# One encoder layer on one core: small steps moved between engines and within the order of the work

## The chip, the core and the metric

The kernel runs on one core of one Trainium2 chip. A core has a matrix engine (TensorE, PE in the profile), a vector engine (VectorE, DVE), a scalar engine (ScalarE, ACT), a general engine (GpSimd, POOL) and SyncE (SP), which here only issues transfers. Each engine takes its instructions in the order in which they were queued and stops at the first one whose operands are not ready. Data lies in SBUF (128 partitions) and the results of matmuls in PSUM. The metric is the device time in microseconds of one execution; it is 901.49 us, the median of 901.3, 901.49 and 904.68.

## The reference

One layer (DEPTH 1) over 512 tokens and 16 learned meta tokens, width 1024:

- h = RMSNorm(x), then one projection h @ W_in gives u (512 columns), q (1024), k and v (256 each) and two gates (1024 each).
- u goes through a bidirectional diagonal complex state-space model with 32 groups of 16 channels and 64 states per direction, then GELU and a gated linear unit.
- q and k are normalized per head of 64 (RMSNorm), rotated by position tables and used in attention: 16 query heads share 4 key heads, the softmax goes over all 528 tokens.
- out = x + W_out(sigmoid(gate_ssm) * (y_ssm @ P_ssm) + sigmoid(gate_attn) * (y_attn @ P_attn)); then an MLP with relu squared (4096 wide) and a last RMSNorm. The meta tokens are dropped at the end.

## The kernel before, in words

All matmuls are in float32 accuracy by a split: each operand is a high part (`split`, line 101: a cast on one engine) plus a low part (the difference, a subtraction on another engine), and `mm3` (line 157) adds three products. So each weight tile needs a DMA, a cast and a subtraction before PE can use it.

`load_w` (line 108) does this for one weight tile. It has two buffers each for the raw tile `wf`, the high part `wh` and the low part `wl`. `W_ENG[0]` says for load number i which engines work: ScalarE casts, and the low part is a subtraction on VectorE or GpSimd, or, where the second entry is None, it is made by ScalarE (negated copy, line 122) and an accumulating DMA that GpSimd issues (line 123). From the state stage on (line 504) the first eight loads go by DMA and the later ones by VectorE.

The stages, in order of time in the profile:

1. Start, to about 60 us. `xnorm` (line 459) normalizes the four 128-row tiles of x and the 16 meta rows: ScalarE squares and sums, VectorE and ScalarE make the reciprocal root (`rsqrt`), VectorE scales (line 479), PE transposes (line 483) and both engines split the result into hTh and hTl. It is called for tile 0, for tile 1 with the meta rows, and for tiles 2 and 3. PE meanwhile projects k (kv_t[0], five row blocks, of which the last is the meta rows), the first 128 columns of u, then v. VectorE also computes the parameters of the state space model (`p_exp`, `p_sincos`); the first instruction of that block (line 568) masks `dd`, the table made from the input ssm_d, which is first read in `ssm_build` (line 785).
2. State projection and scan, about 60 to 226 us. `ssm_build`, `ssm_run` and `ssm_out` make 8 rounds; between them `pump` (line 278) emits matmuls of the fill tasks: the rest of u, the first gate and three tiles of the second gate.
3. Gated linear unit, keys, first two query groups and the projection of y_ssm, about 226 to 300 us. `norm_rope` (line 923) normalizes and rotates k or one group of four query heads; `k_stacks` (line 975) transposes the keys and writes high and low parts Kh and Kl. Each key head is written twice, into partitions 0 to 63 and 64 to 127, since `scores` multiplies a tile that holds the high part of a query head in one half and the low part in the other.
4. Attention, about 300 to 476 us. Per head and block of 128 queries: scores on PE, maximum on VectorE, exp on ScalarE, reciprocal on VectorE, scaling on GpSimd (line 1134), transposes on PE, split on ScalarE and VectorE, and the product with v. The third and fourth query groups and five tiles of the second gate are background work in this stage; the steps of `norm_rope` are then queued in `bgq` and taken out a few at a time (`bg_pop`).
5. From about 476 us: output projections and the MLP.

The order on each engine comes from a scheduler that simulates the whole program: each instruction has a priority by its place in the program, changed by `tc.high_priority`, and `tc.issue_after` holds an instruction behind another one of its engine. A moved line therefore changes the priority of its instructions, and the simulated order of others may change with it. The task list itself is planned by costs written in the code: `pump` advances a clock by 0.33 or 0.65 per step, a task runs when `ready()` holds, and when a task starts, the next ready one has its weights loaded.

The steps that matter here: `rsqrt` (line 165) has a branch for 16 or more columns that starts from an integer trick on VectorE and makes three Newton steps of three VectorE instructions each (lines 179 to 181). In attention `norm_rope` calls it with 16 columns (128x16). The fill list of stage 3 is line 1091, and it runs until line 1092 is satisfied; the list for attention is line 1176. The key halves are written here:

```
for src, cs_ in ((ps, slice(NM, L)), (pm_, slice(L, L + NM)), (pm_, slice(0, NM))):
    for d_ in (a, b_):
        split(src[a], Kh[d_, g, cs_], Kl[d_, g, cs_], S, V)
```

Of the kernel before, what the change touches and what calls it, by code (L numbers as in the profile page):

```python
# [10 lines left out]
F32 = mybir.dt.float32  # L11
# [3 lines left out]
ALU = mybir.AluOpType  # L15
# [9 lines left out]
G = 32  # L25
P16 = 16
# [44 lines left out]
def hybrid_block(ctx, tc, x, meta, w_in, w_glu, w_ssm, w_attn, w_out, w_m1, w_m2,  # L71
# [3 lines left out]
    V, S, Q, PE = nc.vector, nc.scalar, nc.gpsimd, nc.tensor  # L75
# [12 lines left out]
    ident = const.tile([128, 128], F32, name="ident")  # L88
# [3 lines left out]
    W_ENG = [lambda i: (S, Q if i % 2 else V)]  # L92
# [8 lines left out]
    def split(src, h, l, eh, el):  # L101
        a = copy_on(eh, h, src)
        b = el.tensor_tensor(out=l, in0=src, in1=h.bitcast(F32), op=ALU.subtract)  # L103
        return [a.ins, b.ins]
# [57 lines left out]

    rs_ins = []

    def rsqrt(v, n, p=128, name="rs"):

        y, a, t = [small.tile([128, n], F32, tag=f"rs_{c}{n}", bufs=4 if n < 16 else 1 if n > 16 else 2, name=name + c)[:p]
                   for c in "yat"]
        if n < 16:
            rs_ins[:] = [S.activation(out=y, in_=v, func=AF.Abs_reciprocal_sqrt).ins]  # L170
            V.tensor_scalar(out=a, in0=v, scalar1=-0.5, scalar2=None, op0=ALU.mult)
        else:
            V.tensor_scalar(out=t.bitcast(I32), in0=v.bitcast(I32), scalar1=1, scalar2=None,
                            op0=ALU.logical_shift_right)
            V.tensor_scalar(out=y.bitcast(I32), in0=t.bitcast(I32), scalar1=-1.0,
                            scalar2=1597463007.0, op0=ALU.mult, op1=ALU.add)
            V.tensor_scalar(out=a, in0=v, scalar1=-0.5, scalar2=None, op0=ALU.mult)
        for _ in range(1 if n < 16 else 3):
            V.tensor_tensor(out=t, in0=y, in1=y, op=ALU.mult)
            V.tensor_tensor(out=t, in0=t, in1=a, op=ALU.mult)  # L180
            V.scalar_tensor_tensor(out=y, in0=t, scalar=1.5, in1=y, op0=ALU.add, op1=ALU.mult)
        return y
# [55 lines left out]
    dd = sp.tile([P16, G, P16], F32, name="dd")  # L238
# [37 lines left out]
    fill_q, clk, brk, owed, ordered = [], [0.0], [False], [0.0], [False]  # L276
# [180 lines left out]
    xn_ins, xs_ins = [], []  # L457
# [35 lines left out]
    with tc.issue_after(xn_ins[1]):  # L493
        for _ in range(len(bgq) // 2):
            bgq.pop(0)[1]()
        with tc.issue_after(xs_ins[1]):
            bg_flush()
    xnorm((1,), True)
    xnorm((2, 3), False)
    x_st.close()  # L500
    fill_q += [kv_t[0], t_u(0, uTs), kv_t[1]]
    drain()
    nw0 = wcount[0]
    W_ENG[0] = lambda i: (S, V if i - nw0 > 7 else None)


    def tt(a, b, op, o=None):
        o = ptile() if o is None else o
        V.tensor_tensor(out=o, in0=a, in1=b, op=op)
        return o  # L510
# [54 lines left out]
        return sin, cos  # L565

    with tc.issue_after(xn_ins[1]):
        V.tensor_tensor(out=dd, in0=dd, in1=ident[:P16, None, :P16].to_broadcast([P16, G, P16]), op=ALU.mult)
        dt = p_exp(ldt)
        lre = ts(are, -1e-4, ALU.min)  # L570
    mag = p_exp(tt(lre, dt, ALU.mult))
    sn, cs = p_sincos(tt(aim, dt, ALU.mult))
    GP = [128, G, P16]
    sc1, sc2, sc3, sc4 = [pp.tile(GP, F32, name=f"sc{j}") for j in range(4)]
    sc5, sc6 = [gfl[:, 4 * G * j:4 * G * j + 4 * G] for j in range(2)]
# [288 lines left out]
    for i in range(8):  # L864
        c, b = divmod(i, 2)
# [38 lines left out]
    Kh = kp.tile([128, NKV, L + NM], F32R, name="Kh")  # L904
    Kl = kp.tile([128, NKV, L + NM], F32R, name="Kl")
# [17 lines left out]
    def norm_rope(nt, qk, steps=None, buf=0):  # L923
# [6 lines left out]
        st = small.tile([128, 5, 4], F32, tag="st", name="st")[:, :nt]  # L930
# [3 lines left out]
        rr = []  # L934
# [4 lines left out]

        def rs():  # L940
            V.tensor_scalar(out=st, in0=st, scalar1=1.0 / HD, scalar2=EPS, op0=ALU.mult, op1=ALU.add)
            rr.append(rsqrt(st.rearrange("p t h -> p (t h)"), nt * 4).rearrange("p (t h) -> p t h", t=nt))

        def sin_(h):
            n = h.stop - h.start
# [29 lines left out]
    def k_stacks(kr):  # L975
        pm2 = asc()
        for gp in range(2):
            ps = atr()
            pm_ = pm2[:, 16 * gp:16 * gp + 16]
            for t in range(5):  # L980
                n = 128 if t < 4 else 16
                PE.transpose(ps[:, t * 128:t * 128 + 128] if t < 4 else pm_,
                             kr[:n, t, 2 * gp:2 * gp + 2, :].rearrange("p g d -> p (g d)"), ident[:n, :n])
            for o in range(2):
                g = 2 * gp + o
                a, b_ = slice(64 * o, 64 * o + 64), slice(64 - 64 * o, 128 - 64 * o)
                for src, cs_ in ((ps, slice(NM, L)), (pm_, slice(L, L + NM)), (pm_, slice(0, NM))):
                    for d_ in (a, b_):
                        split(src[a], Kh[d_, g, cs_], Kl[d_, g, cs_], S, V)

    stk = {}

# [86 lines left out]
    q_t = [t_qfull(g, qs_[g], None if g > 1 else mmp) for g in range(NKV)]  # L1079
    qT_t = [t_qT(g, qs_[g], None if g else mmp) for g in range(NKV)]  # L1080
# [7 lines left out]
        for m in range(KD):  # L1088
            S.activation(out=t1[:, m, :], in_=t1[:, m, :], func=AF.Sigmoid)
    ss_t = [t_ssm(i) for i in range(4)]  # L1090
    fill_q += [q_t[0], qT_t[0], q_t[1], qT_t[1]] + ss_t
    while any(t in fill_q for t in ss_t + [qT_t[0], q_t[1]]):
        pump(0.1, True)
    mid_st.close()
# [78 lines left out]
    ga_i = iter(ga_t[MG:5])  # L1173
    ordered[0] = True
    for c in ORD:
        fill_q += [next(ga_i)] if c == "g" else [q_t[int(c)], qT_t[int(c)]]
    for qt in range(NT):
        scores(0, qt)
        pend.pop(0)()
# [419 lines left out]
```

## Time and profile before

| | |
|---|---|
| device time, median of three runs | 901.49 us |
| device time of the profiled execution | 908.27 us |
| span of its instructions | 906.4 us |
| PE busy | 854.1 us (94%), 4798 matmuls |
| DVE busy | 677.3 us (75%), 1219 instructions |
| ACT busy | 521.8 us (58%), 914 instructions |
| POOL busy | 192.9 us (21%), 185 instructions |
| mean granted TensorE clock | 0.980 of full speed |

A busy engine is one that has an instruction under way. PE's clock has two levels, 1.2 and 2.4 GHz; a granted clock of 1.00 in a stretch means the upper one all the time, 0.50 the lower one. In a row of a timeline the brackets give the idle time of the engine before the instruction and what ended it.

### The profile page before, as it was taken

Reading aid. Unit: us, or ns where it says so; the run is one execution under the profiler, and the core shown is the slowest. Engines: PE = TensorE matmul, PEld = TensorE weight load, DVE = VectorE, ACT = ScalarE, POOL = GpSimd, SP = SyncE. Lnnn points to the kernel's source line nnn. Section 1 sums busy time; section 2 is a strip of 40 time slices with the busy share of each in tenths; the row PEclk is TensorE's granted clock in tenths of the full one; section 3 lists DMA queues with packets and bytes.
Section 4 is the critical chain, followed back from the end, with each engine's and each line's share of the span. In section 5 each row is a group of like instructions: output and inputs, shape, how many; then the busy total and the mean of one; then the engine's idle time right before and its main releaser. Section 6 shows DMA issues by size and latency. Waiting matters only on the chain.

```text
span 906.4 us, 13080 instructions
## 1 busy us (share of the span) xinstructions
PE 854.1 (94%) x4798; PEld 730.5 (81%) x4798; DVE 677.3 (75%) x1219; ACT 521.8 (58%) x914; POOL 192.9 (21%) x185
## 2 busy tenths in 40 slices
PE   6989999988998889899989999999999999999994
PEld 4988888877987879788868888888888888888884
DVE  7897889868898697877784636847667567776687
ACT  5346686546754566588785345665655555555543
POOL 1001000000220576667544441010100001000000
PEclk9999999979999999999999999999999999999998
DMA  7144632311222010002024343565666666565402
GB/s 239 48 97 102 151 91 77 94 30 47 71 87 77 29 47 24 24 24 71 2 74 134 117 137 103 180 163 139 170 148 155 147 172 161 141 186 129 105 1 93
DMA packets 97473, 92.52 MB, mean 102 GB/s; under 512 B 4465, under 2 KB 79793, under 8 KB 97410
## 3 DMA queue, kind: packets, MB, share of 16 engines
q1 hardware_dynamic: 87824, 69.25, 25.2%
q0 software_dynamic: 5168, 18.40, 10.5%
q10 hardware_dynamic: 4418, 4.04, 1.6%
q8 instruction: 38, 0.62, 0.3%
q14 instruction: 25, 0.20, 0.1%
HBM read 69.03 MB, written 2.10 MB: 78 GB/s over the span
## 4 chain that ended last, share of the span: by engine, by line
PE 73%; DVE 12%; DMA 5%; ACT 5%; issue 4%; POOL 1%; ACTq 0%; DVEq 0%; SPq 0%; POOLq 0%
PE m L161 6%; PE m L160 6%; PE m L159 6%; PE o L160 5%; PE o L159 5%; PE o L161 5%; PE pv L1194 3%; DMA wf<-in_w_in_dram 3%; PE sc L1120 2%; PE atr L1144 2%; PE adp L159 2%; PE adp L160 2%; PE adp L161 2%; DVE wl L125 2%; DMA wl<-wf 2%
## 5 line engine op out<-in xcount | busy, mean ns | idle before, releaser
L98 ACT CAST wh<-wf 128x512 fp32r<-128x512 f32 (+1 forms) x120 | 89.8, 778 | 97.6 <-PE m L160 58.2
L1465 DVE TENSOR_TENSOR ybuf<-o,ybuf 128x1024 f32<-128x1024 f32 x52 | 63.5, 1221 | 67.9 <-PE o L161 67.7
L123 POOL DMA_DIRECT2D wl<-wf x35 | 30.2, 863 | 376.3 <-ACT wl L122 349.5
L161 PE MATMUL m<-h2h,wl 128*128 128x512 f32 (+1 forms) x272 | 102.4, 377 | 0.8 <-DVE wl L125 0.8
L160 PE MATMUL m<-h2l,wh 128*128 128x512 f32 (+1 forms) x272 | 102.5, 377 | 0.2 <-DVE h2l L103 0.2
L159 PE MATMUL m<-h2h,wh 128*128 128x512 f32 (+1 forms) x272 | 102.3, 377 | 0.3 <-ACT h2h L98 0.2
L160 PE MATMUL o<-ol,fh 128*128 128x512 f32 (+1 forms) x216 | 83.2, 385 | 0.0
L159 PE MATMUL o<-oh,fh 128*128 128x512 f32 (+1 forms) x216 | 83.2, 385 | 0.0
L161 PE MATMUL o<-oh,fl 128*128 128x512 f32 (+1 forms) x216 | 83.2, 385 | 0.0
L125 DVE TENSOR_TENSOR wl<-wf,wh 128x512 fp32r<-128x512 f32 (+1 forms) x65 | 57.6, 904 | 16.9 <-ACT wh L98 16.9
L161 PEld LDWEIGHTS m<-h2h,wl 128*128 128x128 f32 x272 | 51.2, 188 | 10.5 <-DVE wl L125 1.2
L159 PEld LDWEIGHTS m<-h2h,wh 128*128 128x128 f32 x272 | 51.1, 188 | 10.2 <-ACT h2h L98 0.5
L160 PEld LDWEIGHTS m<-h2l,wh 128*128 128x128 f32 x272 | 51.2, 188 | 9.7 <-DVE h2l L103 0.4
L1124 DVE TENSOR_REDUCE mx<-sc 128x1 f32<-128x528 f32 x64 | 44.7, 702 | 13.1 <-PE sc L1120 12.4
L103 DVE TENSOR_TENSOR pl<-atr,ph 128x512 fp32r<-128x512 f32 x64 | 43.4, 684 | 9.3 <-ACT ph L98 8.5
L98 ACT CAST ph<-atr 128x512 fp32r<-128x512 f32 x64 | 37.1, 584 | 18.1 <-PE atr L1144 17.6
L159 PEld LDWEIGHTS o<-oh,fh 128*128 128x128 f32 x216 | 40.6, 188 | 8.2
L161 PEld LDWEIGHTS o<-oh,fl 128*128 128x128 f32 x216 | 40.6, 188 | 8.1
L160 PEld LDWEIGHTS o<-ol,fh 128*128 128x128 f32 x216 | 40.6, 188 | 8.0
L1134 POOL TENSOR_TENSOR ea<-zT,rsm 128x528 f32<-128x528 f32 x32 | 34.2, 1067 | 21.3 <-DVE rsm L1133 20.4
L122 ACT ACTIVATE wl<-wf 128x1024 fp32r<-128x1024 f32 x35 | 36.8, 1053 | 0.9 <-PE kvps L160 0.9
L98 ACT CAST oh<-q 128x1024 fp32r<-128x1024 f32 x24 | 25.3, 1056 | 20.0 <-PE o L161 20.0
(403 smaller groups left out, 2506.7 us busy)
## 6 DMA issues: line engine op xcount, KB each, us to landing
wl<-wf POOLq DMA_DIRECT2D x35, 512.0 KB, 4.4
wf<-in_w_in_dram SPq DMA_DIRECT2D x32, 512.0 KB, 3.9
wf<-in_w_m_dram SPq DMA_DIRECT2D x32, 512.0 KB, 4.1
q<-in_w_m_dram SPq DMA_DIRECT2D x32, 512.0 KB, 4.6
ybuf<-in_x_dram SPq DMA_DIRECT2D x8, 512.0 KB, 4.0
wf<-in_w_attn_dram SPq DMA_DIRECT2D x8, 512.0 KB, 3.9
wf<-in_w_out_dram SPq DMA_DIRECT2D x8, 512.0 KB, 3.2
wf<-in_w_ssm_dram SPq DMA_DIRECT2D x4, 512.0 KB, 3.4
```

The source lines that it names most:

```text
L98: return S.copy(out=o, in_=i)
L103: b = el.tensor_tensor(out=l, in0=src, in1=h.bitcast(F32), op=ALU.subtract)
L122: S.activation(out=wl[:, r], in_=wf[:, r], func=AF.Copy, scale=-1.0)
L123: Q.dma_start(out=wl[:, r], in_=wf[:, r], accum_op=ALU.add)
L125: el.tensor_tensor(out=wl[:, r], in0=wf[:, r], in1=wh[:, r].bitcast(F32), op=ALU.subtract)
L159: PE.matmul(out=o, lhsT=lh, rhs=rh, start=first, stop=False, skip_group_check=goes_on)
L160: PE.matmul(out=o, lhsT=lh, rhs=rl, start=False, stop=False, skip_group_check=goes_on)
L161: return PE.matmul(out=o, lhsT=ll, rhs=rh, start=False, stop=last, skip_group_check=goes_on)
L1124: g0 = V.tensor_reduce(out=mx, in_=sc[:, :, :NL], axis=AX.XY, op=ALU.max, negate=True)
L1134: pend.append(lambda: Q.tensor_tensor(out=en, in0=e, in1=rs_.to_broadcast([128, L]), op=ALU.mult))
L1194: PE.matmul(out=pvt[0][:, 256 * f:256 * f + 256], lhsT=vw, rhs=pw, start=left == [8, 9], stop=left == [0, 0])
L1465: V.tensor_tensor(out=x2q[r][h], in0=z, in1=x2q[r][h], op=ALU.add)
```

## The change

Five edits:

1. The meta rows are normalized with tiles 2 and 3 (third call of `xnorm`) and no longer with tile 1.
2. The masking of `dd` moves from the head of the parameter block to behind `p_sincos`, held behind the last scaling instruction of `xnorm`.
3. Of the loads of the state stage the first now has its low part made by VectorE and the ninth by DMA (before: the first eight by DMA).
4. In attention the Newton steps of `rsqrt` run on GpSimd: the product by -0.5 and three steps of four instructions (the step's fused instruction is written as two). The integer start stays on VectorE. The third and fourth query groups are normalized so; the keys and the first two groups are not.
5. `k_stacks` splits each key head into one half only, and ScalarE then copies Kh and Kl as a whole (64 partitions x 544) into the other half. And the third query group is put at the end of the fill list of stage 3, so that its weights are loaded and split when the last tile of the projection of y_ssm starts; its matmuls are still emitted at the first step of attention, before the gates.

```diff
-    def rsqrt(v, n, p=128, name="rs"):
+    def rsqrt(v, n, p=128, name="rs", eng=None):
...
-            V.tensor_scalar(out=a, in0=v, scalar1=-0.5, scalar2=None, op0=ALU.mult)
+            (eng or V).tensor_scalar(out=a, in0=v, scalar1=-0.5, scalar2=None, op0=ALU.mult)
+        if eng is not None:
+            for _ in range(3):
+                eng.tensor_tensor(out=t, in0=y, in1=y, op=ALU.mult)
+                eng.tensor_tensor(out=t, in0=t, in1=a, op=ALU.mult)
+                eng.tensor_scalar(out=t, in0=t, scalar1=1.5, scalar2=None, op0=ALU.add)
+                eng.tensor_tensor(out=y, in0=t, in1=y, op=ALU.mult)
+            return y
...
-    xnorm((1,), True)
-    xnorm((2, 3), False)
+    xnorm((1,), False)
+    xnorm((2, 3), True)
...
-    W_ENG[0] = lambda i: (S, V if i - nw0 > 7 else None)
+    W_ENG[0] = lambda i: (S, V if i == nw0 or i - nw0 > 8 else None)
...
     with tc.issue_after(xn_ins[1]):
-        V.tensor_tensor(out=dd, in0=dd, in1=ident[:P16, None, :P16].to_broadcast([P16, G, P16]), op=ALU.mult)
         dt = p_exp(ldt)
         lre = ts(are, -1e-4, ALU.min)
     mag = p_exp(tt(lre, dt, ALU.mult))
     sn, cs = p_sincos(tt(aim, dt, ALU.mult))
+    with tc.issue_after(xn_ins[-1]):
+        V.tensor_tensor(out=dd, in0=dd, in1=ident[:P16, None, :P16].to_broadcast([P16, G, P16]), op=ALU.mult)
...
-            rr.append(rsqrt(st.rearrange("p t h -> p (t h)"), nt * 4).rearrange("p (t h) -> p t h", t=nt))
+            rr.append(rsqrt(st.rearrange("p t h -> p (t h)"), nt * 4, eng=None if steps is None else Q).rearrange("p (t h) -> p t h", t=nt))
...
-                    for d_ in (a, b_):
-                        split(src[a], Kh[d_, g, cs_], Kl[d_, g, cs_], S, V)
+                    split(src[a], Kh[a, g, cs_], Kl[a, g, cs_], S, V)
+                for k_ in (Kh, Kl):
+                    S.copy(out=k_[b_, g], in_=k_[a, g].bitcast(F32))
...
-    fill_q += [q_t[0], qT_t[0], q_t[1], qT_t[1]] + ss_t
+    fill_q += [q_t[0], qT_t[0], q_t[1], qT_t[1]] + ss_t + [q_t[2]]
...
-        fill_q += [next(ga_i)] if c == "g" else [q_t[int(c)], qT_t[int(c)]]
+        fill_q += [next(ga_i)] if c == "g" else [t for t in (q_t[int(c)], qT_t[int(c)]) if t not in fill_q]
```

## Rows read from the trace of the kernel before

**Rows 1.** Windows of three stages: start and end, length, busy (instructions) per engine, PEclk, DMA

```profile
60.00:226.00 166.00, 156.21 (x990) 133.73 (x989) 139.54 (x262) 100.03 (x203) 7.51 (x21) 0.95 0.38 91
226.00:300.00 74.00, 67.19 (x408) 58.41 (x409) 66.35 (x128) 44.19 (x90) 14.88 (x8) 0.99 0.24 72
300.00:480.00 180.00, 164.95 (x1149) 147.55 (x1149) 136.23 (x258) 127.66 (x273) 108.32 (x94) 0.98 0.14 42
```

**Rows 2.** Timeline of PE at the transposes of tile 1: start, length, bracketed idle before

```profile
18.24 1.39 PE L483 MATMUL xtr<-ident,ybuf 128*128 128x128 f32 x8 [1.72 <-DVE ybuf L479]
```

**Rows 3.** Timeline of DVE, 14.8 to 17.5 us

```profile
14.88 0.17 DVE L473 TENSOR_SCALAR xst<-xst 128x2 f32<-128x2 f32 x1 [0.37 <-ACT t L472]
...
16.30 0.68 DVE L568 TENSOR_TENSOR dd<-dd,ident 16x512 f32<-16x512 f32 x1 [0.83 <-DMA dd<-in_ssm_d_dram]
...
17.44 0.74 DVE L479 SCALAR_TENSOR_TENSOR ybuf<-ybuf,rsy,t 128x512 f32<-128x512 f32 x1
```

**Rows 4.** Groups by line, 8 to 46 us: busy us, mean ns, then idle before

```profile
L472 ACT ACTIVATE t<-t 16x1024 f32<-16x1024 f32 x1 | 1.1, 1056 | 0.0
```

**Rows 5.** Windows of ten us in the start and the state stage

```profile
20.00:30.00 10.00, 9.97 (x63) 9.43 (x63) 7.92 (x27) 3.24 (x8) 0.00 (x0) 0.69 0.01 2
...
60.00:70.00 10.00, 7.95 (x51) 7.51 (x51) 10.00 (x30) 2.92 (x7) 0.88 (x1) 0.83 0.93 209
...
180.00:190.00 10.00, 8.24 (x61) 6.80 (x59) 9.69 (x17) 5.31 (x10) 0.29 (x3) 1.00 0.14 50
190.00:200.00 10.00, 7.96 (x43) 6.73 (x43) 2.70 (x6) 4.01 (x8) 0.14 (x2) 0.67 0.20 42
200.00:210.00 10.00, 10.00 (x38) 8.71 (x38) 8.58 (x12) 5.94 (x14) 0.00 (x0) 0.65 0.06 13
```

**Rows 6.** Timeline of PE at the first product with a low part of the state stage

```profile
63.02 0.39 PE L161 MATMUL ups<-hTh,wl 128*128 128x264 f32 x1 [2.02 <-DMA wl<-wf]
```

**Rows 7.** Timeline of DVE at the ninth load of the state stage

```profile
132.34 1.28 DVE L125 TENSOR_TENSOR wl<-wf,wh 128x512 fp32r<-128x512 f32 x2
```

**Rows 8.** Instructions that write Kl: ns min/median/max, first and last start

```profile
L103 DVE TENSOR_TENSOR Kl<-asc,Kh x16: 159/169/178, 241.2 to 279.9; 64x16 fp32r<-64x16 f32 x16
L103 DVE TENSOR_TENSOR Kl<-atr,Kh x8: 676/689/695, 242.5 to 255.1; 64x512 fp32r<-64x512 f32 x8
```

**Rows 9.** Instructions of line 827, the nearest ScalarE copy by size

```profile
L827 ACT COPY X<-gbuf x8: 620/626/631, 102.6 to 221.4; 64x520 f32<-64x520 f32 x8
```

**Rows 10.** Timeline of PE at the third query group's second half of weights

```profile
299.33 0.58 PE L160 MATMUL adp<-wl,hTh 128*128 128x256 f32 x1 [2.35 <-DVE wl L125]
```

**Rows 11.** Timeline of DVE at the same place

```profile
297.04 2.23 DVE L125 TENSOR_TENSOR wl<-wf,wh 128x512 fp32r<-128x512 f32 x1
```

**Rows 12.** Timeline of DVE, attention: first and last of ten `rsqrt` instructions, groups three and four

```profile
326.43 1.32 DVE L177 TENSOR_SCALAR rsa<-st 128x16 f32<-128x16 f32 x1
...
333.10 0.66 DVE L181 SCALAR_TENSOR_TENSOR rsy<-rst,rsy 128x16 f32<-128x16 f32 x1
...
369.73 0.16 DVE L177 TENSOR_SCALAR rsa<-st 128x16 f32<-128x16 f32 x1
...
375.56 1.07 DVE L181 SCALAR_TENSOR_TENSOR rsy<-rst,rsy 128x16 f32<-128x16 f32 x1
```

**Rows 13.** Windows of twenty us in attention

```profile
320.00:340.00 20.00, 16.47 (x108) 14.20 (x107) 19.25 (x33) 11.65 (x26) 15.18 (x13) 1.00 0.18 53
...
360.00:380.00 20.00, 16.28 (x106) 14.42 (x105) 17.21 (x35) 12.39 (x26) 13.34 (x12) 0.91 0.10 27
380.00:400.00 20.00, 18.87 (x126) 16.52 (x125) 12.94 (x27) 12.58 (x28) 10.45 (x11) 1.00 0.10 27
```

**Rows 14.** Groups of POOL by line and shape: busy us, mean ns, idle before

```profile
L946 POOL TENSOR_TENSOR ybuf<-kvraw,rt 128x1024 f32<-128x1024 f32 x2 | 4.8, 2397 | 35.0 <-DVE Kl L103 25.1 <-DVE st L938 9.8
L950 POOL TENSOR_TENSOR kvraw<-kvraw,rt 128x512 f32<-128x512 f32 x4 | 5.1, 1285 | 0.0
...
L825 POOL MEMSET X<- 64x8 f32 x8 | 0.9, 112 | 107.9 <-PE yo L836 103.3 <-ACT es L773 4.6
```

## The prediction

> **What bounds the kernel now.** I read the windows of the stages first. From about 476 us PE has work without a break and nothing in the change touches that part, so only the first 476 us can move. In the state stage PE is busy 156.21 of 166 us at a granted clock of 0.95, DVE 139.54; in the stage of keys and queries PE 67.19 and DVE 66.35 of 74; in attention PE 164.95 and DVE 136.23 of 180 [rows 1]. PE leads everywhere, but its idle time and its stretches at the lower clock are where microseconds lie, and both come mostly from a late DVE. So I next read PE's waits, and then what DVE does at each.
>
> Four places stand out. First, PE waits 1.72 us at 18.24 for the scaling of tile 1 [rows 2]. DVE is late there because it stood 0.83 us for the DMA of ssm_d and then masked for 0.68 [rows 3], with the squares of the meta rows ahead of the statistics on ACT (1.06 us, [rows 4]). PE then runs at 0.69 of its clock for 10 us [rows 5]. Second, at 63.02 PE waits 2.02 us for the low part of the first weight of the state stage, which comes by DMA [rows 6]; the ten us around it hold 2.05 us of idle PE and a clock of 0.83, with DVE full [rows 5]. Third, the end of the state stage: 1.76 and 2.04 us idle, clocks of 0.67 and 0.65 in 190 to 210 [rows 5]. Fourth, the two places in attention where a query group is normalized: PE idle 3.53 of 20 us in 320 to 340 and 3.72 in 360 to 380, against 1.13 in the next window [rows 13].
>
> **The change part by part.** The sum is a saving, set against the profiled execution's 908.27 us (span 906.4, 1.87 around it). The median of the runs shown is 901.49, so that execution was 0.75% slow; I take the saving off the median.
>
> A. Meta rows and dd at the start. Gone from ahead of tile 1: ACT's square of the meta rows (1.06), the 0.83 stall and the 0.68 mask, together 2.6 us [rows 3, 4]. That is more than PE's wait of 1.72 [rows 2]; what is late next is PE itself, which still works on tile 0's keys until about 16.5. If PE isn't interrupted its clock need not fall, which in 20 to 30 us is worth (1 - 0.69) x 10 = 3.1 us [rows 5]. Upper end 4.8. Lower end 1.7: PE, now early, waits for tiles 2 and 3 and the clock falls there instead; their statistics also carry the meta square now, but start 2.6 us earlier. The meta row's own scaling and transposes are needed only by the last row block of the key projection, and dd first by line 785 in the state stage: hidden. The moved mask costs its 0.68 again in DVE's parameter block, which is full up to 70 us. I take 4.
>
> B. First load of the state stage on DVE. PE's 2.05 us idle plus (1 - 0.83) x 10 = 1.7 at the lower clock can go: 3.75 [rows 5, 6]. DVE pays two half subtractions, 1.28 as in [rows 7], in a stretch where it has no idle time, and what is queued behind them is the building of the first state matrices, for which PE waits next. Ends -1.3 and 3.75; I take 2.5, nearer the PE rows since the wait measured there is the very one that is removed. ACT loses one negated copy, POOL one issue.
>
> C. Ninth load by DMA. DVE gets back 1.28 in a full stretch [rows 7]; ACT and POOL get a copy and an issue. If the DMA is late, PE can lose what the first load lost, 3.75 [rows 5]. Ends -3.75 and 1.3; loads are issued a whole task ahead here, so I take 0.
>
> How much of A and B arrives at 226 us? PE must follow the chain of the eight rounds, in which DVE has 26 us of slack in total [rows 1] but none up to 70 us, and the end of the stage is set by handovers between engines [rows 5]. I pass on half of 6.5: 3.25.
>
> D. Keys. Of 24 pairs of cast and subtraction 12 go. On DVE 4 x 0.689 + 8 x 0.169 = 4.1 us go, in a stage where it is busy 66.35 of 74 [rows 1, 8]. ACT loses as many casts and gains 8 copies of 64x544; scaled from 0.626 for 64x520 each is 0.65, so 5.2 before the casts are taken off [rows 9]; it is busy 44.19 of 74 [rows 1], and that hides it. The cover is gone only if the four copies of the first heads stand in front of the casts of query weights: 4 x 0.65 = 2.6 lost. The added wait is in ACT's order (a copy waits for DVE's last small subtraction of its head); behind it stand casts and projection copies, for which PE waits. PE's idle time in this stage is 6.8 us [rows 1]. Ends -2.6 and 4.1; I take 2.
>
> E. Third query group's weights. PE waits 2.35 us for the second half of that weight [rows 10], whose subtraction took 2.23 us beside GpSimd's scaling [rows 11]. The earlier place in the list raises its priority, but its buffer comes free only with the last products of the y_ssm projection, shortly before the subtraction of [rows 11], in both kernels. So at most the row maximum ahead of it and part of the 2.23 go. Lower end -1.3, two half subtractions (1.28) pushed in front of work that PE waits for; upper end 2.35; I take 1.
>
> F. Newton steps on GpSimd. DVE loses ten instructions per group: 5.3 us in the third (first and last of the ten in [rows 12]) and 3.95 in the fourth. Undisturbed, small ones take 0.17 [rows 8]; those that took 0.66 to 1.32 ran beside a GpSimd instruction. Behind them DVE's queue holds row maxima and splits, for which ACT and PE stand. The excess of PE's idle time over the quiet window is 3.53 - 1.13 = 2.4 and 3.72 - 1.13 = 2.6, and the clock of 0.91 adds 0.09 x 20 = 1.8: upper end 6.8 [rows 13]. GpSimd gains 13 instructions per group. No row shows one of 128x16 there; the nearest are 0.112 us (memset of 8 columns) and 1.285 us (512 columns) [rows 14], so 1.5 to 16.7 us per group. From 1.285 at 512 and 2.397 at 1024 columns the fixed part is 0.17 and a column 0.0022, so 0.21 for 16 columns: I take 2.7 us per group, near the short row. GpSimd has 4.8 and 6.7 us idle in the two windows [rows 13], so it fits; if it doesn't, the scaling of the exponentials queues behind it and 5.4 are lost. The integer start stays on DVE, and the remaining stalls with it. I take half the upper end, 3.5.
>
> The Trainium skill speaks against this step ("SBUF — State Buffer", section Who interferes with whom): GpSimd and VectorE share one pair of ports as an exclusive lock, and a VectorE instruction with two SBUF inputs fully waits for a GpSimd one that reads SBUF. The stretched rows agree. By that rule the lock moves with the work, and the saving of F would be nothing; the rival below carries it.
>
> Sum: 3.25 + 0 + 2 + 1 + 3.5 = 9.75, so 901.49 - 9.75 = 891.7; I say 892.
>
> **The rivals.**
> 1. The start's gain is given back: the rounds wait for DVE, and A and B pass on nothing. For it: DVE is full up to 70 us; against: DVE stands idle 7.3 us in 190 to 200 [rows 5], so it isn't the bound later. 901.49 - 6.5 = 895.0.
> 2. The lock moves with the work: thirteen short GpSimd instructions stretch DVE's neighbours as now four long ones do, F saves nothing. For it the 1.32 and 1.07 against 0.17 [rows 12]; against it, a wait is then at most 0.2 long. 901.49 - 6.25 = 895.2.
> 3. GpSimd's queue becomes the late one in attention, since its Newton chain waits in order for DVE's integer start: F costs 5.4. 901.49 - 6.25 + 5.4 = 900.6. Against it: its idle time in the two windows.
> 4. Slower: the ninth load's low part lands late, as the first does now. PE idles (3.75), the clock falls, that round's results come late, and the stall of the stage's end occurs once more: 1.76 + 2.04 idle and (0.33 + 0.35) x 10 at the lower clock, 10.6 [rows 5]. A and B are gone with it: 901.49 + 14.35 - 6.5 = 909.3. It decides when the DMA lands after PE has finished the task before. For it: one load by DMA does so now [rows 6]; against: that load had no task of its own stage ahead of it, this one has.
> 5. The change doesn't do what it says in E, because the buffer decides: 892.7.
>
> **How the numbers follow.** Forecast 0.50, its own range 886 to 896.5; rival 1 0.14, rival 2 0.10, rival 3 0.10, rival 4 0.13, rival 5 0.03. The upper ends together (4.8, 3.75, 1.3, 4.1, 2.35, 6.8) would give 878, which needs all at once; I let the range begin at 883. Upward it takes in rivals 1, 2, 3 and 5 and ends at 904; rival 4 is left out, and the 16.7 us per group with it. About 0.5%, 4.5 us, is what a measurement here tells from no change. Faster (below 897): forecast, rivals 1, 2 and 5, less 0.03 for their tails, 0.74. Same: rival 3 and the tails, 0.13. Slower: rival 4, 0.13.
>
> **What would show it.** A: line 568 behind line 479 on DVE, tile 1's transposes with no idle PE ahead, a clock near 1 in 20 to 30 us, the key projection's end some 4 us earlier. B: no DMA wait ahead of the first product with wl in 60 to 70. Passing on: the state stage's end (226 us now) 3 us earlier. D: eight subtractions of 64x16 in place of 16. F: 26 new GpSimd instructions of some 0.2 us, PE idle near 2 us in each of the two windows. Wrong would be: the state stage ending no earlier, a GpSimd instruction of 128x16 near 1 us, or new idle PE at the ninth load.

## The result, and the profile after

The changed kernel takes 893.4 us (median of 4 runs, 892.31 to 894.93) against 902.93 for the kernel before in the same runs (901.3 to 904.68): ratio 0.9885, 95% interval 0.9858 to 0.9912. That is 9.5 us, where the sum said 9.75 and the forecast 892. The total is right. The experiments below show that several of its terms are not. (By its ratio the change saves 1.15% of 902.9, or 10.4 us. The ratios go over all runs and lie nearer to the means than to the medians. Where the two differ below, the interval covers both.)

| | before | after |
|---|---|---|
| profiled execution (span), us | 908.27 (906.4) | 892.31 (890.5) |
| mean granted clock | 0.980 | 0.989 |
| start to first `u` copy, us | 41.7 | 39.2 |
| state stage, to the last GELU | 185.3 | 179.9 |
| keys and queries, to the first scores | 60.4 | 57.1 |
| attention, to the last copy of its output | 187.2 | 182.5 |
| new instructions on POOL, 128x16 | none | 26 |

The two profiles lie 15.9 us apart, the medians 9.5: the profiled execution of before was one of its slowest. So the price of a part is taken from ratios of many runs below, and the profiles are asked only where and why.

The windows of the changed kernel that answer to [rows 5] and [rows 13] (start and end, length, busy with count for PE, PEld, DVE, ACT and POOL, PEclk, DMA share, GB/s). The last two are moved with the work: they lie around the integer start of the third and fourth group's root (312.73 and 350.60 us here, 325.30 and 368.59 before) as 320 to 340 and 360 to 380 did in the kernel before:

```profile
20.00:30.00 10.00, 9.09 (x77) 8.47 (x77) 10.00 (x44) 3.17 (x7) 0.00 (x0) 1.00 0.01 2
60.00:70.00 10.00, 9.75 (x68) 8.70 (x67) 7.95 (x25) 5.69 (x12) 0.87 (x1) 1.00 0.72 170
...
190.00:200.00 10.00, 7.15 (x36) 5.91 (x35) 7.41 (x12) 5.18 (x9) 0.00 (x0) 0.74 0.16 33
200.00:210.00 10.00, 10.00 (x48) 8.17 (x47) 9.55 (x24) 3.23 (x7) 0.22 (x2) 0.92 0.11 21
307.43:327.43 20.00, 20.00 (x146) 18.71 (x145) 17.86 (x30) 13.14 (x30) 17.55 (x26) 1.00 0.27 79
342.01:362.01 20.00, 19.28 (x139) 17.30 (x138) 14.73 (x30) 15.56 (x35) 17.01 (x26) 1.00 0.10 27
```

In 20 to 30 us PE now has its full clock (0.69 before); in 60 to 70 it is idle 0.25 us in place of 2.05, again at full clock; at the third group's normalization PE has no idle time in place of 3.53 us, at the fourth's 0.72 in place of 3.72. The end of the state stage (190 to 210) still has 2.85 us of idle time, and less of the lower clock.

PE at tile 1's transposes, at the first product with a low part, and at the third query group (timeline of PE: start, length, bracketed idle before):

```profile
15.93 1.32 PE L490 MATMUL xtr<-ident,ybuf 128*128 128x128 f32 x8 [0.27 <-DVE ybuf L486]
18.41 0.39 PE L159 MATMUL kvps<-wh,hTh 128*128 128x256 f32 x1 [1.16 <-ACT hTh L98]
...
59.81 0.37 PE L161 MATMUL ups<-hTh,wl 128*128 128x264 f32 x1
...
288.26 0.39 PE L160 MATMUL adp<-wl,hTh 128*128 128x256 f32 x1 [2.36 <-DVE wl L125]
```

The wait of [rows 2] is down from 1.72 to 0.27, but behind the transposes PE now waits 1.16 us for their copy by ACT, where it had none before. The wait of [rows 6] is gone. The one of [rows 10] is there to within a hundredth: 2.36 for 2.35.

The new groups on POOL, and what is left of the reciprocal root on DVE (groups by line and shape, 300 to 400 us: busy us, mean ns, idle before):

```profile
L182 POOL TENSOR_SCALAR rst<-rst 128x16 f32<-128x16 f32 x6 | 2.1, 354 | 0.3
L181 POOL TENSOR_TENSOR rst<-rst,rsa 128x16 f32<-128x16 f32 x6 | 1.5, 252 | 0.2
L183 POOL TENSOR_TENSOR rsy<-rst,rsy 128x16 f32<-128x16 f32 x6 | 1.3, 222 | 0.4
L180 POOL TENSOR_TENSOR rst<-rsy 128x16 f32<-128x16 f32 x6 | 1.3, 215 | 0.3
L177 POOL TENSOR_SCALAR rsa<-st 128x16 f32<-128x16 f32 x2 | 0.5, 268 | 0.0
```

```profile
L173 DVE TENSOR_SCALAR rst<-st 128x16 int32<-128x16 int32 x2 | 2.4, 1208 | 0.1
L175 DVE TENSOR_SCALAR rsy<-rst 128x16 int32<-128x16 int32 x2 | 1.4, 696 | 0.0
```

Together 6.7 us for both groups, 3.35 each: the estimate was 2.7. The integer start stayed stretched, as the prediction said.

The writers of `Kl` (ns min/median/max, first and last start), which answer to [rows 8] and [rows 9]:

```profile
L103 DVE TENSOR_TENSOR Kl<-asc,Kh x8: 157/172/178, 232.4 to 251.4; 64x16 fp32r<-64x16 f32 x8
L103 DVE TENSOR_TENSOR Kl<-atr,Kh x4: 683/688/694, 232.7 to 243.8; 64x512 fp32r<-64x512 f32 x4
L998 ACT CAST Kl<-Kl x4: 639/644/647, 238.5 to 251.6; 64x544 fp32r<-64x544 f32 x4
```

Half of the subtractions are gone, and a copy costs 0.644 (0.65 estimated).

### The profile page after: what moved, and what is told of

Same layout as the page of the kernel before. It is cut to its first block, busy times and chain, and to the rows that moved or that the text cites. A ratio compares the mean times of both kernels' runs of the same rounds, so it can differ in the third digit from the quotient of the medians.

```text
span 890.5 us, 13063 instructions
## 1 busy us (share of the span) xinstructions
PE 845.7 (95%) x4798; PEld 722.7 (81%) x4798; DVE 665.2 (75%) x1187; ACT 522.3 (59%) x910; POOL 198.7 (22%) x211
## 3 DMA queue, kind: packets, MB, share of 16 engines
q0 software_dynamic: 5168, 18.40, 10.7%
## 4 chain that ended last, share of the span: by engine, by line
PE 77%; DVE 10%; ACT 5%; issue 3%; DMA 2%; POOL 1%; ACTq 0%; DVEq 0%; POOLq 0%
PE m L161 7%; PE m L160 6%; PE m L159 6%; PE o L161 5%; PE o L159 5%; PE o L160 5%; PE pv L1203 3%; PE sc L1129 3%; PE atr L1153 2%; PE gps L161 2%; PE gps L159 2%; PE adp L159 2%; PE adp L160 2%; PE adp L161 2%; PE gps L160 2%
## 5 line engine op out<-in xcount | busy, mean ns | idle before, releaser
L125 DVE TENSOR_TENSOR wl<-wf,wh 128x512 fp32r<-128x512 f32 (+1 forms) x65 | 59.9, 942 | 13.2 <-ACT wh L98 13.2
L161 PEld LDWEIGHTS m<-h2h,wl 128*128 128x128 f32 x272 | 51.2, 188 | 10.5 <-DVE wl L125 1.3
L159 PEld LDWEIGHTS m<-h2h,wh 128*128 128x128 f32 x272 | 51.1, 188 | 10.1 <-ACT h2h L98 0.5
L103 DVE TENSOR_TENSOR pl<-atr,ph 128x512 fp32r<-128x512 f32 x64 | 43.4, 684 | 14.1 <-ACT ph L98 13.5
L98 ACT CAST ph<-atr 128x512 fp32r<-128x512 f32 x64 | 37.0, 585 | 17.5 <-PE atr L1153 17.1
L161 PEld LDWEIGHTS o<-oh,fl 128*128 128x128 f32 x216 | 40.6, 188 | 8.1
L160 PEld LDWEIGHTS o<-ol,fh 128*128 128x128 f32 x216 | 40.6, 188 | 8.1
L159 PEld LDWEIGHTS o<-oh,fh 128*128 128x128 f32 x216 | 40.6, 188 | 8.0
L1143 POOL TENSOR_TENSOR ea<-zT,rsm 128x528 f32<-128x528 f32 x32 | 34.2, 1069 | 14.8 <-DVE rsm L1142 13.8
L161 PE MATMUL gps<-hTh,wl 128*128 128x512 f32 x88 | 36.0, 409 | 1.2 <-DMA wl<-wf 1.2
L159 PE MATMUL gps<-hTh,wh 128*128 128x512 f32 x88 | 36.6, 416 | 0.3 <-ACT uT L366 0.3
```

The source lines that it names most:

```text
L98: return S.copy(out=o, in_=i)
L125: el.tensor_tensor(out=wl[:, r], in0=wf[:, r], in1=wh[:, r].bitcast(F32), op=ALU.subtract)
L159: PE.matmul(out=o, lhsT=lh, rhs=rh, start=first, stop=False, skip_group_check=goes_on)
L160: PE.matmul(out=o, lhsT=lh, rhs=rl, start=False, stop=False, skip_group_check=goes_on)
L161: return PE.matmul(out=o, lhsT=ll, rhs=rh, start=False, stop=last, skip_group_check=goes_on)
L1143: pend.append(lambda: Q.tensor_tensor(out=en, in0=e, in1=rs_.to_broadcast([128, L]), op=ALU.mult))
```

## The experiments

Each kernel is the one before with one part of the change (A to F are the prediction's names), or the changed one without a part. "Stages" are the four of the table above, in that order, from one profiled execution each. For every stage I also summed, over windows of 2 us, PE's idle time and its loss at the lower clock, (1 - granted clock) x busy. What is left is nearly the same in all kernels (some 31, 167, 57 and 166 us, each within about 1 us), so these two sums hold the larger differences:

| kernel | ratio [95%] | stages, us | idle per stage | lower clock per stage |
|---|---|---|---|---|
| before | 1 | 41.7 / 185.3 / 60.4 / 187.2 | 7.2 / 10.5 / 3.2 / 18.6 | 3.4 / 8.5 / 0 / 3.2 |
| before, once more | one run | 41.3 / 184.7 / 60.4 / 187.3 | 7.5 / 10.1 / 3.2 / 18.6 | 3.4 / 8.4 / 0 / 3.2 |
| after | 0.9885 [0.9858, 0.9912] | 39.2 / 179.9 / 57.1 / 182.5 | 8.0 / 7.5 / 1.2 / 15.4 | 0 / 5.1 / 0 / 1.7 |
| A alone | 1.0041 [1.0020, 1.0061] | 39.5 / 185.6 / 60.4 / 187.2 | 8.1 / 14.1 / 3.2 / 17.3 | 0 / 3.3 / 0 / 4.9 |
| B and C alone | 0.9967 [0.9943, 0.9992] | 41.3 / 176.5 / 59.5 / 185.6 | 7.5 / 8.1 / 2.6 / 17.3 | 3.4 / 1.7 / 0 / 3.1 |
| F alone | 0.9988 [0.9967, 1.0008] | 40.2 / 180.5 / 60.5 / 185.9 | 7.8 / 10.5 / 3.3 / 16.2 | 1.6 / 3.1 / 0 / 4.8 |
| D alone | 0.9963 [0.9941, 0.9986] | 41.6 / 178.2 / 57.5 / 187.1 | 7.0 / 10.1 / 1.1 / 18.5 | 3.4 / 1.7 / 0 / 3.1 |
| E alone | 1.0023 [0.9999, 1.0047] | 38.8 / 184.5 / 60.4 / 190.7 | 7.2 / 10.1 / 3.2 / 19.2 | 0 / 8.2 / 0 / 4.4 |
| E and F | 0.9948 [0.9923, 0.9973] | 40.4 / 180.6 / 60.3 / 183.5 | 8.2 / 10.7 / 3.3 / 15.3 | 1.7 / 3.0 / 0 / 1.7 |
| without A | 0.9868 [0.9844, 0.9892] | 40.0 / 176.2 / 57.1 / 183.2 | 7.8 / 8.0 / 0.9 / 15.5 | 1.7 / 1.7 / 0 / 1.7 |
| without F | 0.9966 [0.9943, 0.9989] | 39.0 / 179.4 / 57.1 / 193.6 | 7.6 / 8.6 / 1.2 / 17.9 | 0 / 3.1 / 0 / 9.6 |
| without E | 0.9929 [0.9902, 0.9955] | 39.3 / 179.5 / 57.1 / 188.3 | 7.8 / 8.6 / 1.2 / 16.8 | 0 / 3.3 / 0 / 4.7 |
| without D | 0.9886 [0.9855, 0.9918] | 40.7 / 179.3 / 61.3 / 179.7 | 8.2 / 8.4 / 3.7 / 13.6 | 1.7 / 3.3 / 0 / 0 |
| without A and C | 0.9907 [0.9882, 0.9933] | 40.2 / 181.0 / 57.5 / 182.0 | 7.9 / 12.3 / 1.1 / 15.3 | 1.6 / 1.5 / 0 / 0 |

The parts alone add up to 1.6 us saved (3.7 - 3.0 - 1.1 - 3.3 + 2.1 = -1.6, each (ratio - 1) x 902.9), the whole saves 10.4 by its ratio. The change is no sum of its parts.

The granted clock of every run is on record too, so the lower clock can be averaged over runs. (1 - granted clock) x span is 16.1 us in the kernel before (75 runs), 10.5 in the changed one (4 runs), 16.3 without F (12), 13.6 without E (6), 17.7 with F alone (12) and 13.5 with E and F (12). So of the 10.7 us by which the means of before and after differ here, 5.6 are the clock and 5.1 the rest. F alone saves 2.6 us apart from the clock and loses 1.6 by it.

**The kernel before, unchanged, once more.** 

> The kernel before, unchanged, for a second profile. The profiled execution of before took 908.27 us against a median of 901.49. Theory: the 5 to 7 us too many stand at one place, as a stretch at the lower clock in the state stage (190 to 210) or in attention (360 to 380), and this profile, near 902, ends that stage earlier: last GELU near 222 to 227, first scores near 282 to 287, last attention copy near 469 to 475. Rival: they are spread over all stages, a few tenths each.


Measured: 907.32 us, granted clock 0.980; 29 runs of the kernel before beside it and its neighbours had a median of 903.5, from 900.73 (clock 0.987) to 908.18 (0.980). The stretches of the table come out within 0.6 us, so this profile is a fair pair for the first one. Both come from the slow end of the range, so where a faster execution of this kernel saves its time isn't shown.

**A alone.**
```
-    xnorm((1,), True)
-    xnorm((2, 3), False)
+    xnorm((1,), False)
+    xnorm((2, 3), True)
...
-        V.tensor_tensor(out=dd, in0=dd, in1=ident[:P16, None, :P16]...
...
+    with tc.issue_after(xn_ins[-1]):
+        V.tensor_tensor(out=dd, in0=dd, in1=ident[:P16, None, :P16]...
```


> Only the start: meta rows with tiles 2 and 3, dd behind p_sincos. Theory (parts add up, half of the start passes on): first copy of u 2.5 us earlier, whole 2 to 4 us faster, 898 to 900. Rival (the rounds wait for VectorE): 0, 901 to 903, PE idle longer in 60 to 210. Third theory (the start is the whole cause of what the state stage gained): 7 to 8 faster, near 894.


Measured: 906.54 us against 903.5, 0.4% slower. The first `u` copy stands at 39.5 for 41.7, with no loss at the lower clock ahead of it (3.4 before) and 0.9 us more idle time. That is not A's alone: the kernel with E alone, which leaves the start in its old order and waits 1.59 us for tile 1, has no loss there either and is at 38.8. Over the profiles the old start gives 38.8 to 41.7 (nine), the new one 39.0 to 40.7 (five); the averages are 40.6 and 39.5. The state stage's idle time grows from 10.5 to 14.1. PE's waits from 45 to 226 us (us in total, times, longest), first the kernel before, then A alone:

```profile
PE kt L779 <- DVE W L754: 3.2, 2, 1.7
PE yo L836 <- ACT X L828: 2.4, 2, 1.7
...
PE kt L779 <- DVE W L752: 0.6, 1, 0.6
```

```profile
PE kt L780 <- DVE W L755: 3.9, 2, 2.2
PE yo L837 <- ACT X L829: 3.1, 2, 1.7
...
PE kt L780 <- DVE W L753: 1.9, 2, 1.5
```

The waits for `W`, which DVE casts in each round of the state stage, grow from 3.8 to 5.8 us, and those for `X` by 0.7. The last three of them end at 187.5, 193.2 and 195.3 us, those of the kernel before at 185.6, 190.3 and 192.5: `W` comes 2 to 3 us later than it did, although the first `u` copy was 2.2 us earlier. What rival 1 said of the rounds is what happened to A. PE's order in the whole stage changes as well, so how much of it is DVE's time and how much the planner's new order isn't separated.

**B and C alone.**
```
-    W_ENG[0] = lambda i: (S, V if i - nw0 > 7 else None)
+    W_ENG[0] = lambda i: (S, V if i == nw0 or i - nw0 > 8 else None)
```


> Only the loads: the first low part of the state stage on VectorE, the ninth by DMA. Theory: the wait of 2.0 us at 63 and the stretch at the lower clock behind it go, and half passes on: 1 to 2 us faster, 900 to 901. Rival: VectorE's 1.28 us put the state matrices back as much: 0, within 1 us. Third: the ninth load's DMA is waited for, 2 to 4 us slower.


Measured: 901.76 us, ratio 0.9967: 3.0 us faster. The state stage is 176.5 us, idle 8.1 for 10.5. The wait of 2.02 us at the first load is gone; later waits for loads by DMA are 1.4 us in sum for 0.4. So B with C reaches the stage's end without A. Of the 8.8 us by which the stage is shorter in this profile, 6.8 are the lower clock (1.7 for 8.5), which the last section finds in a kernel with an unchanged stage as well.

**Without A.** The changed kernel with A's two edits undone. 

> The whole change without its start: meta rows and dd as before. The start alone was 3.7 us slower than before. Theory (it costs alone what it costs in company): about 4 us faster than the changed kernel, 889 to 890. Rival (the start pays only with the first load on VectorE, which removes the wait that it runs into): 3 to 6 us slower than the changed kernel, 896 to 899.


Measured: 892.29 us, 0.9868. The intervals overlap with the whole change's 0.9885, so neither a gain nor a loss by A can be told here; the middle values differ by 1.5 us against it. This is the lowest ratio of all kernels run, but it isn't shown to be faster than the change as it is.

**Without A and C: the first load on DVE, the ninth left there too.**
```
+    W_ENG[0] = lambda i: (S, V if i == nw0 or i - nw0 > 7 else None)
```


> The change without its start, and with VectorE making both the first and the ninth low part (of the loads only the first differs from before). Without the start the ratio was 0.9868. Theory (all that the loads gain comes from the wait at the first): ratio 0.986 to 0.988, state stage ends as without the start, near 216. Rival (VectorE's time at the ninth load counts): 1.3 us or more slower than without the start, ratio 0.989. Third: faster, since no DMA is waited for at the ninth load: 0.985.


Measured: 896.72 us, 0.9907, against 0.9868 without A alone; that is 0.39% or 3.5 us for C. The intervals overlap slightly, and the two ran on different chips; the traces bear it out. PE's waits from 45 to 226 us, first without A and C, then without A:

```profile
PE kt L786 <- DVE W L761: 3.9, 2, 2.2
PE yo L843 <- ACT X L835: 1.7, 1, 1.7
PE kt L786 <- DVE W L759: 1.6, 3, 0.7
```

```profile
PE yo L841 <- DMA T<-gbuf: 3.0, 1, 3.0
...
PE kt L786 <- DVE W L759: 0.3, 1, 0.3
```

With the ninth load's 1.28 us [rows 7] left on DVE, PE waits 5.5 us for `W`; without it 0.3. In 180 to 200 us PE is busy 15.16 us with it and 16.98 without, both at a clock of 0.91. The low part of the ninth load itself is waited for nowhere: the two DMA waits for `wl` (0.9 and 0.5 us) stand at 85.4 and 110.9 us and are in both kernels, while the subtraction that C removes stands at 130.5 and 131.8. New with C is one wait of 3.0 us for `T` at 192.46, smaller than what went. The waits that went stood 50 us behind the subtraction (2.2 us at 184.6 and 1.7 at 193.0 are the longest), and the order differs on DVE from 130.0 us on, on PE from 137.3. So that C pays is measured; whether by DVE's 1.28 us or by the order that the planner makes of it is open.

**D alone.**
```
-                    for d_ in (a, b_):
-                        split(src[a], Kh[d_, g, cs_], Kl[d_, g, cs_], S, V)
+                    split(src[a], Kh[a, g, cs_], Kl[a, g, cs_], S, V)
+                for k_ in (Kh, Kl):
+                    S.copy(out=k_[b_, g], in_=k_[a, g].bitcast(F32))
```


> Only the keys: second half rows copied by ScalarE. Theory: 2 us faster, about 901 against 903.5; first scores 2 us earlier. Rival (VectorE is not what the stage waits for): 0, first scores where they were. Third (non-additive: most of the whole gain is here): 5 or more faster.


Measured: 900.8 us against 904.93, ratio 0.9963, 3.3 us. The stage of keys and queries goes from 60.4 to 57.5, its idle time from 3.2 to 1.1.

**Without D.** 

> The whole change with both halves of the keys split as before. The keys alone had a ratio of 0.9963, their stage took 57.5 us against 60.4. Theory (additive, as VectorE is full in that stage): the stage takes 60.4 again, ratio 0.992. Rival (the gain of the keys needs the earlier place or is replaced by it): stage 57 to 58, ratio 0.9885.


Measured: 893.94 us, 0.9886, the same as the whole change. The stage takes 61.3 us without D (57.1 with it), and PE waits 2.8 us in it for a `Kl` subtraction; but attention takes 179.7 in place of 182.5, 13.6 idle for 15.4. In company no gain of D can be told: the order of the background work in attention differs, and what D saves ahead of it is lost in it in these two profiles.

**F alone.**
```
+def rsqrt(v, n, p=128, name="rs", eng=None):
...
+        if eng is not None:
+            for _ in range(3):
+                eng.tensor_tensor(out=t, in0=y, in1=y, op=ALU.mult)
...
+            rr.append(rsqrt(..., nt * 4, eng=None if steps is None else Q)...
```


> Only the Newton steps of the third and fourth query groups on GpSimd. Theory: PE idles less at the two places of attention, 3 to 4 us faster, 898 to 899; GpSimd's new instructions take about 0.2 us each. Rival (the port moves with the work): 0, 901 to 903. Rival (GpSimd is the late queue): 3 to 5 us slower.


Measured: 903.75 us against 903.5, 0.9988 [0.9967, 1.0008]: nothing that can be told from no change. From the first row maximum of the fourth head to that of the fifth it takes 14.3 us in place of 18.8; the next four take 11.7, 12.4, 15.3 and 12.1 in place of 9.8, 10.1, 16.8 and 11.8, and 3.0 of the 4.5 us are given back.

**Without F.** 

> The whole change with the Newton steps left on VectorE. Alone they saved 1.1 us. Theory of the prediction: 3.5 us lost, 897. Rival (they save what they save alone): 894 to 895.


Measured: 901.59 us, 0.9966. Among the other parts F is worth 0.0081, 7.3 us. Attention took 193.6 us, of which 9.6 are lost at the lower clock in this one execution. It isn't an odd one: over the 12 runs the mean granted clock is 0.982, against 0.988 in the changed kernel's four. By the means, 5.9 of 7.7 us come by the clock.

**E alone.**
```
-    fill_q += [q_t[0], qT_t[0], q_t[1], qT_t[1]] + ss_t
+    fill_q += [q_t[0], qT_t[0], q_t[1], qT_t[1]] + ss_t + [q_t[2]]
...
-        fill_q += [next(ga_i)] if c == "g" else [q_t[int(c)], qT_t[int(c)]]
+        fill_q += [next(ga_i)] if c == "g" else [t for t in (q_t[int(c)], qT_t[int(c)]) if t not in fill_q]
```


> Only the third query group's earlier place in the list. Theory: 1 us faster, about 902.5, the wait of 2.35 us ahead of the first product with its low part shorter. Rival (the buffer decides): 0, same wait. Third: 3 us or more faster, because the scheduler's order of the stage changes with it.


Measured: 905.58 us against 904.93, 1.0023 [0.9999, 1.0047]. The wait of [rows 10] is untouched (timeline of PE):

```profile
295.62 0.58 PE L160 MATMUL adp<-wl,hTh 128*128 128x256 f32 x1 [2.35 <-DVE wl L125]
```

PE's order is the old one up to 336.9 us of the kernel before. What E does do, by the code: in the loop that drains the y_ssm tasks the last call has budget left when the last of them ends, and spends it on the third group's first step (0.33 by the planner's clock). In the trace the background work then stands where it stood up to 41 us after the first scores, and the fourth group's projection starts 49.0 us after them instead of 51.4. Alone that makes attention 3.5 us longer in the profile.

**E and F together.** 

> Two parts together: Newton steps on GpSimd and the third group's earlier place. Alone they changed the time by a ratio of 0.9988 and 1.0023. Theory (the two belong together: the earlier place shifts the third group's normalization, and only with GpSimd's Newton steps does attention keep up): attention, from the first scores to the last copy of the output, takes 183 us against 187.2 before and 190.7 with the earlier place alone, and the ratio is near 0.994. Rival (parts add): 1.001, attention 189 us.


Measured: 900.91 us against 904.53, 0.9948 [0.9923, 0.9973]: 4.7 us, where the two alone add up to +1.0. The eighth head's maximum comes 84.4 us after the first head's, against 88.5 before, 86.6 with F alone and 90.7 with E alone.

**Without E.** 

> The whole change without the third group's earlier place. Theory (belongs together with the Newton steps): attention 186 us as with the Newton steps alone, 3 to 4 us slower than the changed kernel, ratio to before near 0.993. Rival (the earlier place costs attention 3.5 us in any company): 3 us faster than the changed kernel, ratio 0.985.


Measured: 898.32 us, 0.9929, so E is worth 0.0044 or 4.0 us in company. By the means 3.1 of 4.8 us come by the clock.

Where E and F meet is seen in the windows of 20 us around the third and fourth group's root, moved with the work as in the section on the result (PE's idle time + loss at the lower clock, us):

| kernel | third group | fourth group |
|---|---|---|
| before | 3.5 + 0 | 3.7 + 1.6 |
| F alone | 0.4 + 0 | 3.1 + 3.0 |
| E alone | 2.4 + 0 | 3.7 + 2.1 |
| without E | 0.3 + 0 | 2.7 + 3.0 |
| without F | 1.9 + 1.7 | 3.7 + 2.1 |
| E and F | 0 + 0 | 0.7 + 0 |
| after | 0 + 0 | 0.7 + 0 |

F clears the third group's place by itself; the fourth's is cleared only by both.

What F does is read from the timeline of DVE where the third group is normalized: `wl` split, row maxima (`mx`), the statistics and the root's integer start. First the kernel before, of which [rows 12] showed the first and last Newton instruction, then the changed one:

```profile
318.80 2.14 DVE L125 TENSOR_TENSOR wl<-wf,wh 128x512 fp32r<-128x512 f32 x2
320.86 1.31 DVE L1124 TENSOR_REDUCE mx<-sc 128x1 f32<-128x528 f32 x2
...
325.30 1.22 DVE L173 TENSOR_SCALAR rst<-st 128x16 int32<-128x16 int32 x1
...
330.80 0.70 DVE L1124 TENSOR_REDUCE mx<-sc 128x1 f32<-128x528 f32 x1
```

```profile
306.22 2.14 DVE L125 TENSOR_TENSOR wl<-wf,wh 128x512 fp32r<-128x512 f32 x2
308.28 1.31 DVE L1133 TENSOR_REDUCE mx<-sc 128x1 f32<-128x528 f32 x2
...
312.73 1.22 DVE L173 TENSOR_SCALAR rst<-st 128x16 int32<-128x16 int32 x1
313.98 1.20 DVE L175 TENSOR_SCALAR rsy<-rst 128x16 int32<-128x16 int32 x1
315.09 0.69 DVE L1133 TENSOR_REDUCE mx<-sc 128x1 f32<-128x528 f32 x1
```

Up to the integer start both are alike to 0.02 us. Then the next maximum stands 5.5 us behind it in the kernel before and 2.36 in the changed one: 3.1 us of Newton steps had stood ahead of a maximum for which the exponentials and PE wait. On POOL the same steps lie between the scalings, from 315.12 to 327.27 us, longer than the 7.3 us that they took on DVE, but PE doesn't idle meanwhile (timeline of POOL, the changed kernel):

```profile
315.12 0.28 POOL L177 TENSOR_SCALAR rsa<-st 128x16 f32<-128x16 f32 x1
315.37 1.06 POOL L1143 TENSOR_TENSOR zT<-rt,rsm 128x528 f32<-128x528 f32 x1
316.40 0.21 POOL L180 TENSOR_TENSOR rst<-rsy 128x16 f32<-128x16 f32 x1
```

## Why the prediction was right, step by step

**The total** was right: 9.5 us by the medians, 10.4 by the ratio, for 9.75. The reading behind it held too: all of it lies ahead of the output projections (behind the last attention copy both kernels take 431.8 us), in PE's idle time and lower clock. But the terms were 3.25 + 0 + 2 + 1 + 3.5, and what each part is worth in the company of the others is another row: some 0 for A, about 3.5 for C, 0 for D, 4.0 for E and 7.3 for F. These overlap and don't add up either. That errors of both signs met in a sum so near the measured one is luck.

**A: the failed step is "I pass on half of 6.5".** The start itself gained 2.2 us with A alone, for the 4 taken: the wait for tile 1 went, but PE's idle time ahead of that copy rose from 7.2 to 8.1, and the clock in 20 to 30 us rose to 1.00. That clock can't be put down to A: it is 0.69 to 0.83 in eight of the nine profiles with the old start, but 1.00 in the ninth (E alone), and 0.87 in one of the five with the new one. None of the gain arrived. The prediction argued that DVE has 26 us of slack over the stage; PE's longer waits for `W` show that slack over a stage says nothing of the moments at which PE wants an input. A should have been passed on at 0, as rival 1 had it; B with C did pass on 3.0 us.

**B: right in place.** The DMA wait of 2.02 is gone from all seven profiles with the load on DVE, and the clock in 60 to 70 is 1.00 in them; with the load by DMA it is 0.83 in six and 1.00 in one (A alone). How much of it alone reaches the end wasn't measured by itself: B and C alone give 3.0, and no kernel has B as its only change.

**C: the failed step is "so I take 0".** Its ends were -3.75 and 1.3. The upper end priced only DVE's 1.28 us, but with the subtraction left in place PE waits 5.5 us for `W` in later rounds, against 0.3, and the kernel takes about 3.5 us more. Rival 4 fell: at the ninth load PE doesn't wait for the DMA at all.

**D: right alone, mis-sized in company.** 3.3 us alone for the 2 taken, and ACT's copies were hidden. The whole loses no gain that can be told without D; the prediction summed the stage's gain and didn't ask what attention does with an earlier start.

**E: the failed step is "part of the 2.23 go".** The wait stays; rival 5 was right that the buffer decides. Its conclusion, that E is worth nothing, was wrong: the slot that E moves is worth 4.0 us beside F. Alone it gains nothing, and attention was longer in its profile.

**F: right in mechanism, mis-sized.** POOL's 3.35 us per group for 2.7 fit its idle time (it is busy 17.55 and 17.01 of 20 us in the two windows), so rival 3 is out. Alone F gives 1.1 (not told from 0), in company 7.3, most of it by the clock, for 3.5 taken. The prediction said that row maxima stand behind the Newton steps, and they did; what it lacked is that the fourth group's place in the background decides whether the 4.5 us won at the third stay: with F alone that place costs 6.1 us where it cost 5.3, with E beside it 0.7.

Rival 2, the lock that moves with the work, fell. The third group's two integer instructions still take 1.2 us on DVE beside POOL's long instructions; the fourth's second one, beside a Newton step of 0.26 us on POOL, takes 0.19. Two of DVE's 128x256 instructions of the rotation take 0.41 and 0.42 beside such steps at 353.7 us, where others take 1.2 to 1.3 beside a scaling; there a step on POOL took 0.41 for 0.25. These are few rows. The maxima say nothing on it, since they keep their 0.7 us beside the long scalings too. The Trainium skill ("SBUF — State Buffer", section Who interferes with whom) says that of two instructions that need the shared pair of ports the second waits until the whole first one has ended. The rows agree, and beside instructions of 0.2 to 0.35 us that wait is short.

The signs named beforehand: clock near 1 in 20 to 30, no DMA wait in 60 to 70, 8 small subtractions and 26 POOL instructions came true; PE idle near 2 us in the two windows came to 2.48 and 2.42, but by luck: the normalizations had moved 13 and 18 us ahead out of them, and where they now stand the idle time is 0 and 0.72. The key projection ended 2.5 us earlier (34.4 for 36.9) and not some 4. The state stage ended earlier in the profiles (227 to 219 us), though 3.4 of that is the clock (8.5 to 5.1) and as much again the clock of the start, which the last section finds to change from one execution to the next. No new idle PE stands at the ninth load.

## What to carry to other kernels

An engine that is full on average isn't the bound: before passing a gain on, look at which wait ends last at the next handover, and don't take an instruction's own length for the upper end of what its move is worth: 1.28 us taken off DVE came with a gain of about 3.5, whether by their time or by the order that followed. Where a planner or a list of due times orders background work, parts of a change are not additive, so time the whole with one part left out as well as the part alone: here the parts alone saved 1.6 us, the whole 10.4. Between two single profiles, take the lower-clock loss out before reading a stage's price, and move the windows with the work that you compare: the same window shows other work once something ahead of it is shorter.

## What the runs showed of the hardware that was not expected

The same program order runs through the same stage with different clocks. F, D, E, and E with F leave the instructions of the state stage on PE, DVE, ACT and POOL in the order of the kernel before (in its trace the first difference stands at 326.4, 247.2, 336.9 and 326.4 us; the stage ends at 227). Still that stage took 180.5, 178.2, 184.5 and 180.6 us against 185.3 and 184.7. The windows of 20 us behind the idle stretch, for the kernel before, D alone and E alone:

```profile
180.00:200.00 20.00, 16.20 (x104) 13.53 (x102) 12.39 (x22) 9.32 (x18) 0.43 (x4) 0.84 0.17 46
200.00:220.00 20.00, 20.00 (x92) 16.62 (x92) 16.73 (x27) 9.24 (x18) 0.22 (x2) 0.82 0.19 59
```

```profile
180.00:200.00 20.00, 16.19 (x121) 13.84 (x120) 14.54 (x25) 8.91 (x18) 0.21 (x2) 1.00 0.16 38
200.00:220.00 20.00, 17.60 (x103) 14.14 (x102) 19.38 (x33) 15.13 (x29) 0.22 (x2) 1.00 0.17 55
```

```profile
180.00:200.00 20.00, 16.20 (x100) 14.50 (x98) 12.01 (x21) 8.32 (x16) 0.21 (x2) 0.74 0.13 27
200.00:220.00 20.00, 18.27 (x88) 14.44 (x88) 15.68 (x28) 11.81 (x23) 0.22 (x2) 0.92 0.17 52
```

Each has the same 3.8 us of idle PE in 180 to 200; after it the clock is at its upper level throughout in D alone and falls towards the lower one in the others. The loss in that stage is 1.7 us here, 8.2 to 8.5 there. 29 runs of the kernel before reach from 900.73 (granted clock 0.987) to 908.18 (0.980), about the same distance. So the some 6 us of [rows 5]'s loss in 190 to 210, which rival 4 priced as the stage's own, aren't fixed by the program. Nor are they rare: of 75 runs of the kernel before, 32 have a granted clock of 0.976 to 0.981 (0.980 in the profile) and 14 one of 0.987 or more, and D alone, whose profile had 0.987, has a mean of 0.982 over its 12 runs, the same as the kernel before. The start shows it too: in the old order its loss is 3.4, 1.6 to 1.7 or 0 us. What decides it wasn't found.
